# A whole-network kernel in split fp32: one weight piece split per call of the routine, one piece beyond the one in use

## The chip, the cores and the metric

The kernel runs on one core of one Trainium2 chip. The metric is the device time of one execution in microseconds (us), as the median of several runs.

## What is computed

The reference runs two blocks of two layers each over one sequence of 256 tokens with 1024 channels, all in fp32. What matters here is that every layer is a chain of a norm and large matrix products:

```python
def rmsnorm(x, g):
    y = xf * lax.rsqrt(jnp.mean(xf * xf, axis=-1, keepdims=True) + RMS_EPS)
    return (y * g.astype(jnp.float32)).astype(x.dtype)
...
        h = h + mixed
        h = h + squared_relu_mlp(rmsnorm(h, norm_mlp[i]), mlp_w_up[i], mlp_w_down[i])
        ple_gate = jax.nn.sigmoid(rmsnorm(h, norm_ple[i]) @ ple_w_gate[i])
        h = h + ple_gate * (p[i].astype(h.dtype) @ ple_w_proj[i])
    return rmsnorm(h, norm_final)
...
        h = h + 0.5 * _swiglu(_rmsnorm(h, ffn1_norm[layer]), ffn1_w_in[layer], ffn1_w_out[layer])
        u = _rmsnorm(h, mix_norm[layer])
...
        h = h + 0.5 * _swiglu(_rmsnorm(h, ffn2_norm[layer]), ffn2_w_in[layer], ffn2_w_out[layer])
```

The mixers of the first block are a short convolution (layer 0) and a dilated attention (layer 1); those of the second are an S5 state space mixer (layer 0) and a sparse attention with three branches (layer 1), whose keys and values come from one projection (kv) after layer 0. The PLE is the gated term with `ple_w_gate`.

## The kernel before

**Weights.** All large weights are cut into 292 pieces, used in one fixed order (`PLAN`). A piece is 128 x 2048 fp32, 1 MB: either 256 columns of a matrix with 1024 rows ("cols") or 256 rows of one with 1024 columns ("rows"). Twelve of them belong to S5 and are not split. The products have to be more exact than a single pass gives, so each weight and each activation is split into a high part (rounded to the format fp32r) and a low remainder, and a product is three matmuls, hi·hi, lo·hi and hi·lo (`mm3`, L362, L363, L364). A piece is 48 matmuls of 128 x 256.

**Splitting.** `split` takes the next pieces in order. For each it opens two pairs of half tiles (`split_open`), and for each half (128 x 1024) ACT writes the high part whi (L289) and DVE the remainder wlo = raw − whi (L290):

```python
            nc.scalar.activation(hi.t[c], rc, AF.Copy)
            nc.vector.tensor_sub(lo.t[c], rc, hi.t[c].bitcast(F32))
```

The tiles lie in rings: three raw pieces, six halves of whi and six of wlo, so three pieces of each. SP starts the load of a raw piece as soon as the ring lets it.

**Who asks for splits.** `piece()` is called once for each piece that is used, number i. Its `fetch` asks for all pieces below i + 3 to be split (`ahead`), within a cap, and for loads up to i + 6. While a norm is pending, the fetch is kept for later:

```python
        if 0 < len(self.todo) < 4 and self.n_split >= i + 2:
            self.late.append(lambda: self.behind(fetch))
        else:
            fetch()
```

**Norms.** The rows of a layer's input are not scaled before the product; the product is scaled behind it by R, a reciprocal root that is the same for all channels of a token. So the first pieces of a stage run while R is still being made: sums of squares on TensorE (`norm_ssq`, L513), rmean on DVE (L523), the power on GpSimd (rcol, L503), dg on GpSimd (L534), a matmul that spreads it over the partitions (L537), and R, a copy by ACT (L539). `norm_at` puts these steps into `todo`, and `norm_step`, called after every second k of a piece, takes one; when the list is empty, everything in `late` is issued, the kept fetches in order behind what was issued on each engine up to then (`behind`). After R the first outputs are scaled: L544 on DVE (e), then in the ffn stages silu on ACT (L882), a scaling on GpSimd (L883), the product with the second half on DVE (L887), and its own split into hh and hl (L438, L439) for the down product. An ffn copies its very first product out of the accumulator on ACT (L875), before R is there. In PSUM there are three accumulators "acc", four "big" and one "misc".

**The order on the engines.** The kernel's text is not the order of execution: a scheduler with a simulated time line orders the instructions of each engine, within the dependencies, the rings and the places where `in_order` forbids it. Each engine then works through its list in that order.

**S5.** `n_split` jumps over the twelve S5 pieces, three pieces are split ahead of time by `split_open(3)`, and at the end of the first update `split(self.n_use + 2)` (L1319) asks for the pieces that follow.

Of the kernel before, what the change touches and what calls it, by code (L numbers as in the profile page):

```python
# [132 lines left out]
PLAN = plan()  # L133
# [89 lines left out]
class Ker:  # L223
# [17 lines left out]
    def load(self, i):  # L241
        nc = self.nc
        while self.n_load < min(i, len(PLAN)):
# [22 lines left out]
            self.raw[n] = t  # L266
            self.n_load += 1

    def split(self, i):
        while self.n_split < min(i, len(PLAN)):  # L270
            todo = self.split_open(1)
            for c in range(2):
                self.split_half(todo, c)
# [896 lines left out]
    def s5(self, upd):  # L1170
# [112 lines left out]
        def presplit(c):  # L1283
            with self.in_order():
                if c == 0:
                    split.extend(self.split_open(3))
                self.split_half(split, c)
# [25 lines left out]
        def upd2(j):  # L1313
            if j == 0:
                accs.extend(self.cols_open("s5_w_glu_2", 0, (256 * i, 256 * i + 128), ahead=3 - i) for i in range(3))
                for ks in (range(4), range(4, 8)):
                    for a in accs:
                        self.cols_part(x, a, ks)
                self.split(self.n_use + 2)  # L1319
            elif j == 1:  # L1320
                a = self.cols_open("s5_w_glu_2", 0, (768, 896))
                self.cols_part(x, a, range(8))
                accs.append(a)
            s = bp.tile([128, 2, S], F32, name="sZ")
            ac.activation(s, accs[j][0], AF.Sigmoid)
            v.tensor_tensor(s, s, Y[0][:, 2 * j:2 * j + 2], op=OP.mult)
            v.tensor_tensor(self.h[j], self.h[j], s, op=OP.add)

        self.cap = len(PLAN)
        return self.norm_feed(upd2, ("ffn2_norm_2", 0))  # L1330


# [562 lines left out]
```

## Time and profile before

| | |
|---|---|
| median of 3 runs | 1885.36 us (1885.01 to 1886.57) |
| the profiled execution | 1886.62 us |
| its span, first to last instruction | 1884.8 us |
| mean granted clock of TensorE | 0.984 |
| TensorE (PE) busy | 1826.6 us, 97% of the span |
| VectorE (DVE) busy | 1292.8 us, 69% |
| ScalarE (ACT) busy | 956.5 us, 51% |
| GpSimd (POOL) busy | 465.3 us, 25% |
| mean transfer rate | 183 GB/s |

Busy time says how much an engine works, not whether somebody waits for it. The waits of an engine say that: which instruction stood idle, and which instruction of another engine ended the wait. The granted clock tells at what share of its full speed TensorE ran in a stretch.

### The profile page before, as it was taken

Reading aid. Unit: us, or ns where it says so; the run is one execution under the profiler, and the core shown is the slowest. Engines: PE = TensorE matmul, PEld = TensorE weight load, DVE = VectorE, ACT = ScalarE, POOL = GpSimd, SP = SyncE. Lnnn points to the kernel's source line nnn. Section 1 sums busy time; section 2 is a strip of 40 time slices with the busy share of each in tenths; the row PEclk is TensorE's granted clock in tenths of the full one; section 3 lists DMA queues with packets and bytes.
Section 4 is the critical chain, followed back from the end, with each engine's and each line's share of the span. In section 5 each row is a group of like instructions: output and inputs, shape, how many; then the busy total and the mean of one; then the engine's idle time right before and its main releaser. Section 6 shows DMA issues by size and latency. Waiting matters only on the chain.

```text
span 1884.8 us, 36094 instructions
## 1 busy us (share of the span) xinstructions
PE 1826.6 (97%) x15242; PEld 1800.5 (96%) x15242; DVE 1292.8 (69%) x1647; ACT 956.5 (51%) x1438; POOL 465.3 (25%) x391
## 2 busy tenths in 40 slices
PE   8999999899999999998999889999999999999999
PEld 8999999899999999998999888999999999899998
DVE  6879987787777788767655585555686556775554
ACT  4455556454445555556444364444565445764442
POOL 2110012655664332211101211110153113421110
PEclk9999999899999999999999989999999999899999
DMA  6565666443343476665555845755455553344452
GB/s 229 205 211 190 218 206 203 149 164 136 134 157 135 175 252 232 224 195 208 201 191 182 284 190 177 242 181 187 162 183 198 179 189 101 56 165 179 179 180 88
DMA packets 80657, 344.72 MB, mean 183 GB/s; under 512 B 8214, under 2 KB 34570, under 8 KB 44656
## 3 DMA queue, kind: packets, MB, share of 16 engines
q1 hardware_dynamic: 79344, 339.33, 51.4%
q0 software_dynamic: 1008, 2.91, 0.5%
q8 instruction: 119, 1.95, 0.4%
q14 instruction: 42, 0.34, 0.1%
q10 hardware_dynamic: 144, 0.20, 0.0%
HBM read 328.73 MB, written 17.86 MB: 184 GB/s over the span
## 4 chain that ended last, share of the span: by engine, by line
PE 77%; DVE 8%; POOL 5%; issue 4%; ACT 3%; DMA 2%; SPq 0%; POOLq 0%; ACTq 0%; DVEq 0%
PE acc L364 15%; PE acc L363 15%; PE acc L362 15%; PE big L364 8%; PE big L363 8%; PE big L362 8%; DVE wlo L290 3%; POOL qkt L767 2%; POOL qks L764 2%; ACT whi L289 1%; POOL qkc L766 1%; PE acc L1720 1%; DMA bias<-zb 1%; DMA s5wi<-wi 1%; ACT qh L438 1%
## 5 line engine op out<-in xcount | busy, mean ns | idle before, releaser
L290 DVE TENSOR_TENSOR wlo<-raw,whi 128x1024 fp32r<-128x1024 f32 x558 | 709.4, 1282 | 312.4 <-ACT whi L289 309.1
L289 ACT ACTIVATE whi<-raw 128x1024 fp32r<-128x1024 f32 x558 | 581.2, 1056 | 540.5 <-PE acc L363 279.6
L362 PE MATMUL acc<-xh,whi 128*128 128x256 f32 x2096 | 597.0, 286 | 10.5 <-ACT xh L441 3.6
L364 PE MATMUL acc<-xh,wlo 128*128 128x256 f32 x2096 | 597.3, 286 | 5.3 <-DVE wlo L439 3.1
L363 PE MATMUL acc<-xl,whi 128*128 128x256 f32 x2096 | 596.3, 285 | 1.9 <-DVE xl L442 1.8
L362 PEld LDWEIGHTS acc<-xh,whi 128*128 128x128 f32 x2096 | 404.7, 193 | 13.1 <-ACT xh L441 3.8
L364 PEld LDWEIGHTS acc<-xh,wlo 128*128 128x128 f32 x2096 | 404.9, 193 | 7.7 <-DVE wlo L439 3.9
L363 PEld LDWEIGHTS acc<-xl,whi 128*128 128x128 f32 x2096 | 405.1, 193 | 2.6 <-DVE xl L442 2.0
L363 PE MATMUL big<-hl,whi 128*128 128x256 f32 x1216 | 344.1, 284 | 0.0
L364 PE MATMUL big<-hh,wlo 128*128 128x256 f32 x1216 | 342.9, 284 | 0.0
L362 PE MATMUL big<-hh,whi 128*128 128x256 f32 x1216 | 342.4, 283 | 0.0
L363 PEld LDWEIGHTS big<-hl,whi 128*128 128x128 f32 x1216 | 232.8, 191 | 1.1 <-issue 1.1
L364 PEld LDWEIGHTS big<-hh,wlo 128*128 128x128 f32 x1216 | 232.0, 191 | 1.5 <-issue 1.5
L362 PEld LDWEIGHTS big<-hh,whi 128*128 128x128 f32 x1216 | 232.2, 191 | 0.2 <-issue 0.2
L883 POOL TENSOR_TENSOR e<-e,R 128x512 f32<-128x512 f32 x44 | 74.0, 1682 | 554.0 <-ACT e L882 544.9
L363 PE MATMUL acc<-yl,whi 128*128 128x256 f32 x720 | 203.2, 284 | 0.7 <-DVE yl L488 0.6
L364 PE MATMUL acc<-yh,wlo 128*128 128x256 f32 x720 | 203.1, 284 | 0.0
L362 PE MATMUL acc<-yh,whi 128*128 128x256 f32 x720 | 202.3, 285 | 0.4 <-ACT yh L474 0.4
L363 PEld LDWEIGHTS acc<-yl,whi 128*128 128x128 f32 x720 | 138.0, 192 | 1.3 <-DVE yl L488 1.3
L362 PEld LDWEIGHTS acc<-yh,whi 128*128 128x128 f32 x720 | 137.5, 193 | 1.0 <-ACT yh L474 0.6
L364 PEld LDWEIGHTS acc<-yh,wlo 128*128 128x128 f32 x720 | 138.1, 192 | 0.1
L482 POOL TENSOR_TENSOR sq<-sq,sqt 128x512 f32<-128x512 f32 x27 | 42.0, 1554 | 138.5 <-ACT sqt L481 137.9
(440 smaller groups left out, 2609.9 us busy)
## 6 DMA issues: line engine op xcount, KB each, us to landing
raw<-in_wst SPq DMA_DIRECT2D x277, 1024.0 KB, 4.9
s5wo<-b SPq DMA_DIRECT2D x8, 512.0 KB, 5.8
s5wi<-wi SPq DMA_DIRECT2D x16, 256.0 KB, 5.2
s5to<-s5k SPq DMA_DIRECT2D x32, 128.0 KB, 3.9
bias<-zb SPq DMA_DIRECT2D x16, 256.0 KB, 4.6
cbt<-zb SPq DMA_DIRECT2D x4, 900.0 KB, 8.6
raw<-s5to SPq DMA_DIRECT2D x6, 512.0 KB, 6.1
raw<-in_wst SPq DMA_DIRECT2D x4, 512.0 KB, 8.0
```

Of the source, the lines that this page charges most:

```text
L289: nc.scalar.activation(hi.t[c], rc, AF.Copy)
L290: nc.vector.tensor_sub(lo.t[c], rc, hi.t[c].bitcast(F32))
L362: mm(out, lh, rh, start=first, stop=False, skip_group_check=True)
L363: mm(out, lh, rl, start=False, stop=False, skip_group_check=True)
L364: mm(out, ll, rh, start=False, stop=last, skip_group_check=True)
L438: nc.scalar.activation(hi, src, AF.Copy)
L482: nc.gpsimd.tensor_tensor(self.sq, self.sq, s, op=OP.add)
L764: nc.gpsimd.tensor_tensor(s, s, bc(self.rS), op=OP.mult)
L766: nc.gpsimd.tensor_tensor(c, t[:32], bc(self.rC), op=OP.mult)
L767: nc.gpsimd.tensor_tensor(t[:32], c, s, op=OP.add)
L883: nc.gpsimd.tensor_tensor(T[i], T[i], self.bc2(self.R), op=OP.mult)
L1720: nc.tensor.matmul(o[:, dst], w, t[lp][e][:, b, src], start=False, stop=(b == 1 and kb == 1 and i == 2), skip_group_check=True)
```

## The change

`split` takes one piece per call at most, in place of all pieces up to the number asked for; both halves of that piece are still split in the call. And the request behind the first S5 update is for one piece beyond `n_use` in place of two. All requests stay as they are otherwise; since a stage begins with one call per piece, the split pieces are one fewer in the program at a given call than before, i + 2 after call i in place of i + 3, and the condition with which `piece()` keeps a fetch for later reads that number. A blank line is added as well, so the change's line numbers stand one above those of before from L269 on.

```diff
@@ -266,8 +266,9 @@
             self.raw[n] = t
             self.n_load += 1
 
+
     def split(self, i):
-        while self.n_split < min(i, len(PLAN)):
+        if self.n_split < min(i, len(PLAN)):
             todo = self.split_open(1)
             for c in range(2):
                 self.split_half(todo, c)
@@ -1316,7 +1317,7 @@
                 for ks in (range(4), range(4, 8)):
                     for a in accs:
                         self.cols_part(x, a, ks)
-                self.split(self.n_use + 2)
+                self.split(self.n_use + 1)
             elif j == 1:
                 a = self.cols_open("s5_w_glu_2", 0, (768, 896))
                 self.cols_part(x, a, range(8))
```

How that moves instructions is seen in three places. First DVE in the PLE of layer 0, from the step rmean of its norm on; e are the products scaled by R, four of them, pp the projection they are added to. Before:

```order
L523 TENSOR_SCALAR rmean<-misc 128x2
L544 TENSOR_TENSOR e_3978<-acc,R 128x512
L544 TENSOR_TENSOR e_4047<-acc,R 128x512
L290 TENSOR_TENSOR wlo<-raw,whi 128x1024 x5
L544 TENSOR_TENSOR e_4060<-acc,R 128x512
L705 TENSOR_TENSOR e_4049<-e_4049,pp_3555 128x512
L706 TENSOR_TENSOR h_72<-h_72,e_3980 128x512
L290 TENSOR_TENSOR wlo<-raw,whi 128x1024
L706 TENSOR_TENSOR h_73<-h_73,e_4049 128x512
L290 TENSOR_TENSOR wlo<-raw,whi 128x1024
L544 TENSOR_TENSOR e_4073<-acc,R 128x512
```

and now:

```order
L291 TENSOR_TENSOR wlo<-raw,whi 128x1024 x2
L524 TENSOR_SCALAR rmean<-misc 128x2
L291 TENSOR_TENSOR wlo<-raw,whi 128x1024 x2
L545 TENSOR_TENSOR e_3970<-acc,R 128x512
L545 TENSOR_TENSOR e_4039<-acc,R 128x512
L291 TENSOR_TENSOR wlo<-raw,whi 128x1024
L706 TENSOR_TENSOR e_4041<-e_4041,pp_3547 128x512
L707 TENSOR_TENSOR h_72<-h_72,e_3972 128x512
L545 TENSOR_TENSOR e_4052<-acc,R 128x512
L707 TENSOR_TENSOR h_73<-h_73,e_4041 128x512
L291 TENSOR_TENSOR wlo<-raw,whi 128x1024
```

Of the block of five halves behind the first two scaled products, one is left; the others stand ahead of them.

Second ACT at the start of the attention: sqt are the squares for the norm, R its result, qh the high part of a query. Before:

```order
L481 ACTIVATE sqt<-h_75 128x512
L433 ACT_TABLE_LOAD
L433 ACTIVATE tab<-ones 128x1
L539 ACTIVATE R<-misc 128x256
L438 ACTIVATE qh_4207<-qkt 128x512
L289 ACTIVATE whi<-raw 128x1024 x6
L438 ACTIVATE qh_4265<-qkt 128x512
```

and now:

```order
L290 ACTIVATE whi<-raw 128x1024 x2
L475 ACTIVATE xh_3751<-h_75,small 128x256
L475 ACTIVATE xh_3752<-h_75,small 128x256
L482 ACTIVATE sqt<-h_75 128x512
L434 ACT_TABLE_LOAD
L434 ACTIVATE tab<-ones 128x1
L290 ACTIVATE whi<-raw 128x1024 x3
L540 ACTIVATE R<-misc 128x256
L290 ACTIVATE whi<-raw 128x1024 x2
L439 ACTIVATE qh_4209<-qkt 128x512
```

Three halves stand between the table and R and two between R and the first query, where there were none.

Third ACT behind the final norm of the first block, at the start of ffn1 of layer 0. Before:

```order
L433 ACT_TABLE_LOAD
L433 ACTIVATE tab<-ones 128x1
L875 ACTIVATE e_10435<-acc 128x512
L539 ACTIVATE R<-misc 128x256
L882 ACTIVATE e_10458<-e_10456 128x512
L289 ACTIVATE whi<-raw 128x1024 x6
L882 ACTIVATE e_10589<-e_10587 128x512
L438 ACTIVATE hh<-e_10458 128x512
L539 ACTIVATE R_10485<-misc 128x256
```

and now:

```order
L434 ACT_TABLE_LOAD
L434 ACTIVATE tab<-ones 128x1
L290 ACTIVATE whi<-raw 128x1024
L876 ACTIVATE e_10427<-acc 128x512
L290 ACTIVATE whi<-raw 128x1024 x4
L540 ACTIVATE R<-misc 128x256
L883 ACTIVATE e_10460<-e_10458 128x512
L883 ACTIVATE e_10581<-e_10579 128x512
L439 ACTIVATE hh<-e_10460 128x512
L439 ACTIVATE hh<-e_10581 128x512
```

The six halves behind the first silu are gone from there; five stand ahead of R, and both silu follow R at once.

## Rows read from the trace of the kernel before

**Rows 1.** Waits of TensorE: total us, times, longest.
```profile
PE big L362 <- ACT whi L289: 5.7, 3, 3.1
...
PE acc L362 <- ACT xh L441: 3.6, 1, 3.6
...
PE acc L362 <- ACT whi L289: 2.6, 2, 2.3
PE acc L362 <- DVE e L544: 2.4, 1, 2.4
...
PE acc L364 <- DVE wlo L290: 2.1, 2, 1.1
...
PE acc L363 <- DVE xl L442: 1.8, 1, 1.8
...
PE big L364 <- DVE wlo L290: 1.0, 1, 1.0
```
**Rows 2.** Windows: us, busy of PE, PEld, DVE, ACT, POOL, PEclk, DMA, GB/s.
```profile
328.00:340.00 12.00, 9.22 (x61) 8.69 (x60) 11.81 (x18) 8.24 (x17) 4.15 (x2) 0.86 0.77 275
348.00:364.00 16.00, 11.87 (x73) 11.14 (x72) 11.86 (x14) 7.21 (x9) 11.79 (x8) 0.79 0.16 56
855.00:872.00 17.00, 11.58 (x76) 11.18 (x76) 16.89 (x27) 12.07 (x28) 0.12 (x1) 0.80 0.59 211
1138.00:1150.00 12.00, 8.73 (x57) 8.26 (x57) 7.96 (x8) 7.74 (x10) 2.65 (x3) 0.86 0.19 67
1336.00:1348.00 12.00, 9.43 (x62) 8.93 (x61) 8.69 (x9) 6.06 (x7) 1.54 (x4) 0.86 0.37 117
1181.00:1187.00 6.00, 6.00 (x52) 6.00 (x52) 3.38 (x4) 2.64 (x3) 2.14 (x2) 1.00 0.56 201
```
**Rows 3.** Waits of ACT: total us, times, longest.
```profile
ACT whi L289 <- PE acc L363: 279.6, 170, 2.7
ACT whi L289 <- PE big L363: 122.0, 86, 2.7
...
ACT R L539 <- PE misc L537: 76.6, 10, 10.6
```
**Rows 4.** Time line of ACT, attention start: start, us, instruction, [idle before <-releaser].
```profile
348.84 0.38 ACT L539 ACTIVATE R<-misc 128x256 f32<-128x256 f32 x1 [7.13 <-PE misc L537]
353.98 0.63 ACT L438 ACTIVATE qh<-qkt 128x512 fp32r<-128x512 f32 x1 [4.75 <-POOL qkt L767]
354.51 5.78 ACT L289 ACTIVATE whi<-raw 128x1024 fp32r<-128x1024 f32 x6
```
**Rows 5.** Time line of ACT behind R, at ffn2 of layer 0 and at kv.
```profile
1142.25 5.77 ACT L289 ACTIVATE whi<-raw 128x1024 fp32r<-128x1024 f32 x6
...
1338.85 5.78 ACT L289 ACTIVATE whi<-raw 128x1024 fp32r<-128x1024 f32 x6
```
**Rows 6.** Time line of DVE in the PLE of layer 0.
```profile
318.76 1.29 DVE L544 TENSOR_TENSOR e<-acc,R 128x512 f32<-128x512 f32 x2 [4.87 <-ACT R L539]
319.97 6.87 DVE L290 TENSOR_TENSOR wlo<-raw,whi 128x1024 fp32r<-128x1024 f32 x5
...
331.43 0.68 DVE L544 TENSOR_TENSOR e<-acc,R 128x512 f32<-128x512 f32 x1
```
**Rows 7.** Page, part 5: busy us, mean ns of one, idle before and releaser.
```profile
L290 DVE TENSOR_TENSOR wlo<-raw,whi 128x1024 fp32r<-128x1024 f32 x558 | 709.4, 1282 | 312.4 <-ACT whi L289 309.1
L289 ACT ACTIVATE whi<-raw 128x1024 fp32r<-128x1024 f32 x558 | 581.2, 1056 | 540.5 <-PE acc L363 279.6
```
**Rows 8.** Time lines of PE and POOL, ffn1 of layer 0.
```profile
880.65 0.59 PE L537 MATMUL misc<-dg,ones 128*128 128x256 f32 x2
...
883.13 1.28 POOL L883 TENSOR_TENSOR e<-e,R 128x512 f32<-128x512 f32 x1 [4.94 <-ACT e L882]
```
**Rows 9.** Group of L534 (ns min/median/max), and time lines of POOL and DVE there.
```profile
L534 POOL TENSOR_TENSOR dg<-cst,rcol x11: 612/613/1161, 23.7 to 1697.1; 128x256 f32<-128x256 f32 x11
...
885.15 0.97 POOL L534 TENSOR_TENSOR dg<-cst,rcol 128x256 f32<-128x256 f32 x1
...
884.39 1.25 DVE L290 TENSOR_TENSOR wlo<-raw,whi 128x1024 fp32r<-128x1024 f32 x1
```

## The prediction

> **What bounds the kernel now.** I read the waits of TensorE first. TensorE is busy nearly all the span, so a change pays only by closing its idle stretches, or by opening new ones. The seven rows that bear on splits and norms [rows 1] hold 5.7 + 3.6 + 2.6 + 2.4 + 2.1 + 1.8 + 1.0 = 19.2 us. Where each falls I took from the windows [rows 2], one per place with the granted clock beside it:
>
> - PLE of layer 0 (332 us): the 2.4 on DVE's L544.
> - attention start (355 us): 3.1 on whi, then the 1.0 on wlo.
> - final norm into ffn1 of layer 0 (860 to 886 us): 3.6 on ACT's xh and 1.8 on DVE's xl, then 0.3 on whi and 1.1 on wlo.
> - ffn2 of layer 0 (1143 us): 2.3 on whi, 1.0 on wlo.
> - kv projection (1340 us): 5.7 − 3.1 = 2.6 on whi.
>
> Each place pays twice. After the idle time the granted clock is lower: 0.86, 0.79, 0.80, 0.86 and 0.86 in these windows, against 1.00 in an undisturbed one [rows 2]; 1.00 is the level of 2.4 GHz, and the windows mix it with 1.2. The shortfall, window times (1 − clock), is time lost at the lower level: 12 × 0.14 = 1.7, 16 × 0.21 = 3.4, 17 × 0.20 = 3.4, 1.7 and 1.7 us.
>
> All five have one cause, seen on ACT and DVE next. While a norm is pending, `piece` puts the fetch of later weights behind R (L539). So ACT stands idle before R, 76.6 us at 10 norms [rows 3], and right after it, or after the first output, issues a whole block of splits. At the attention start it idles 7.13 us before R and 4.75 before qh, and only then runs six halves in 5.78 us [rows 4]; TensorE waits for the first. At ffn2 and at kv six halves follow R in the same way [rows 5]. At the PLE the block stands on DVE: five halves, 6.87 us, ahead of the L544 that TensorE waits for [rows 6]; before the final norm the same five-half block delays the h from which xh and xl come.
>
> **The change part by part.** *One piece per call.* At the start of a stage the lead in the program falls from two pieces beyond the one in use to one. No instruction is added or removed; the counts on all five engines are equal. In the long ffn stretches the order on ACT and DVE reads the same before and after, since the buffers set it: whi waits 279.6 us for TensorE to free a half while acc matmuls run and 122.0 while big ones do [rows 3]. Cost there: zero. The cover is those 401.6 us of waiting; were it gone, one half (1.06 us on ACT, 1.28 on DVE [rows 7]) would be exposed per piece.
>
> *The condition.* With one piece of lead, `n_split >= i + 2` is false when a norm is pending, so the fetch is issued at once. This is the part that moves time. In the order, two to seven halves that stood behind R now stand ahead of it at the norms, on ACT and on DVE, with the SP loads that their freed raw buffers trigger. The idle time that they enter is there: 76.6 us in 10 norms, 7.7 each; seven halves take 7 × 1.06 = 7.4 on ACT. By place:
>
> - PLE: from the first pair of L544 to the fourth one it took 331.43 − 318.76 = 12.7 us [rows 6]. Now two halves run between rmean and that pair, in DVE's idle 4.87, and from pair to fourth stand three halves (1.2 each back to back) and eleven operations of 0.4 to 0.65: some 10.1, so 2.6 sooner; the wait was 2.4. Gain 2.4 + 1.7 = 4.1.
> - attention start: five halves stand before qh where none did. Gain 3.1 + 1.0 + 3.4 = 7.5; less 0.5, as part of the slow stretch lies in the second wait, and less 1, since norm and first head's transposes stand 24 and 49 matmuls later in the order and something of this is late. Gain 6.0.
> - ffn2: four halves ahead of R. Gain 2.3 + 1.0 + 1.7 = 5.0.
> - kv: six halves ahead of R. Gain 2.6 + 1.7 = 4.3.
> - final norm: gross 3.6 + 1.8 + 0.3 + 1.1 + 3.4 = 10.2, less 0.9 for the slow stretch inside the second wait: 9.3. But here the order takes something back. L537, which makes R, stands 192 matmuls into the stage, where it stood at 123. At 0.12 us a matmul (52 of them touch a busy window of 6.00 us, [rows 2]) that is 8.3 us more work ahead of it. The next piece needs the acc buffer of the second one, which L887 frees after R. From L537 to L883 takes 883.13 − 880.65 = 2.48 us, L883 1.28 [rows 8], L887 some 0.7 (as the other DVE operations on 512 columns): 4.5. TensorE stands for about 4.3 of it, and I add 1.7 for the clock, as at the other places with 2 to 3 us. Gain 9.3 − 6.0 = 3.3.
>
> *S5.* `n_use + 1` in place of 2 at L1319 moves the split of one glu piece a little later; the order there shows swaps of neighbours. Bounds: two halves earlier or later, −2.3 to +2.3 us; I take 0, since the waits of S5 in the trace are on other names. The interleave of background work in both mlps shifts too; TensorE has no idle time on splits there. Bounds −2 to +2, taken as 0.
>
> *A cost that the rows price.* Splits ahead of R run beside the GpSimd operations that make R. dg (L534) took 0.61 us in the median, but 0.97 at 885.15, where a wlo split ran until 885.64 [rows 9]. I add nothing at four places, since TensorE does not wait for R there. The Trainium skill (SBUF — State Buffer, SBUF: two separate sides) says that DVE and GpSimd share a pair of ports, which a DVE operation with two SBUF inputs, as a wlo split is, locks for its whole length against a GpSimd operation that reads SBUF; the stretched dg agrees. By that rule rcol and dg could each wait out one split, and the gain at the final norm would be some 2.6 us less by the durations above.
>
> Sum: 4.1 + 6.0 + 3.3 + 5.0 + 4.3 = 22.7 us. Profiled execution 1886.62 − 22.7 = 1863.9; it stands 1.3 above the median of 1885.36, so by the median 1862.7. I forecast **1863**.
>
> **The rivals.**
>
> 1. *Half the gain.* The splits come early, but the attention start and the final norm stay held by the chain of R (rmean, rcol, dg, L537, R, then L544 and GpSimd). For it: at both, L537 is later in the order. Against: 24 matmuls are 2.9 us, and the whi that TensorE waited for needs no R. Left are PLE, ffn2 and kv: 13.4 us, 1886.6 − 13.4 = 1873, by the median 1872.
>
> 2. *No change.* The wait is for TensorE to free a half, so a split issued earlier only waits earlier. For it: the 401.6 us of such waits [rows 3]. Against: at the five places ACT idles for R or qh, not for a buffer. 1885.
>
> 3. *Slower: R is held by the splits ahead of it.* ACT takes instructions in order. If a half ahead of R waits for a buffer that matmuls behind the norm free, R waits with it, and all that scales by R. It decides where more halves stand ahead of R than are free. The price is the final norm's, 4.3 + 1.7 = 6.0 us, at 10 norms [rows 3], 60, less 22.7 kept: +37, 1923. For it: up to seven halves ahead of R against a ring of six. Against: right after R six halves run without a gap [rows 5], so their buffers were free by then, and a half ahead of R could hold it only until that point. The Trainium skill (TensorE: Matmul & The Clock Gate, Architectural detail) says that the queues of ACT and DVE are strictly first in, first out, by which a blocked half would hold R; the rows agree in so far as ACT's rows stand in the order's sequence.
>
> 4. *It does not do what it says.* The words speak of half a piece; the code still splits both halves, one piece per call. That by itself changes no number above. But after the nsa mixer the program's lead is used up, each call splitting its own piece. If ACT ran in that order, about 37 pieces would each expose 1.06 + 1.28 us, 86 us: 1971. Against: the order rows there are the same as before.
>
> **How the numbers follow.** Forecast 0.55, half the gain 0.27, no change 0.09, R held 0.07, lead used up 0.02. The first two make faster 0.82; same is 0.09, slower 0.09. A measurement tells 0.2%, 3.8 us, from no change. Range: its low end is the forecast less the 6.0 taken back at the final norm, less 2 to 3 for S5 and the mlps: 1854. Its high end is the half gain, 1872, plus one new wait of 6.0 and the 2 of the mlps: 1880. What lies outside is no change and the slower cases, 0.18.
>
> **What would show it.** Right: ACT's whi runs ahead of R and the idle time before R is well under 76.6 us; the rows whi → big and whi → acc (5.7, 2.6) nearly vanish; windows at 332, 355, 1143 and 1340 us have clock over 0.95; one new wait of 3 to 5 us near 880 us on DVE's L887. Wrong: TensorE waits on R, on qh or on L544 where it waited on whi, or the whi waits reappear in stretches where the order did not change. The forecast fails if clock losses stay though the waits go, or if new waits open in the mlps.

## The result and the profile after

The changed kernel took 1860.43 us in the median of 4 runs (1859.66 to 1861.85), against 1885.96 us before (4 runs); the ratio is 0.9865, 95% interval 0.9848 to 0.9882, so 25.5 us or 1.35% less. The forecast was 1863.

First the waits of TensorE after, in the view of [rows 1] (total us, times, longest; the change's lines stand one higher):

```profile
PE big L818 <- ACT p L813: 8.2, 3, 2.9
PE big L1229 <- DVE sX L1265: 6.6, 2, 5.5
...
PE acc L363 <- ACT e L883: 3.1, 1, 3.1
...
PE acc L363 <- DVE e L654: 2.3, 1, 2.3
...
PE big L364 <- DVE ql L440: 1.4, 1, 1.4
```

None of the seven rows of [rows 1] is left: not one wait on a whi or wlo that `split` makes, on xh or xl of the final norm, or on L544 of the PLE. Those 19.2 us are gone whole. (The very first piece is split elsewhere, in `first_feed`; TensorE still waits for it, 4.6 us before and 5.1 now.) Three smaller waits are new: e (L883) behind the final norm, e (L654) at the start of the second mlp, ql in the attention. Two more rows need a look. One is p, in the heads of the attention; before, it read:

```profile
PE big L817 <- ACT p L812: 7.6, 4, 2.8
```

It is 0.6 us longer now: a wait of 2.5 us at head 0 (380 us) is new, and one of 2.8 at 452 us of before is gone. The other, sX in S5, was 3.2 us with 2.6 as the longest, beside 3.2 us at the same line on issue (waits for which the profile shows no releaser), of which 0.4 are left; the waits in S5 come to 12.1 us before and 12.4 now. All waits of TensorE add up to some 53 us before and 40 now, so about half of the 25.5 us is idle time. The other half is the clock: its mean rose from 0.984 to 0.991, and span times (1 − clock) fell from 30.2 to 16.7 us.

Next the windows of the five places in the profile after, each with the same columns as [rows 2], and then three with a wait in them (the final norm's R, the second mlp, head 0 of the attention):

```profile
322.00:336.00 14.00, 14.00 (x119) 14.00 (x118) 14.00 (x19) 10.11 (x17) 2.82 (x2) 1.00 0.49 168
342.00:358.00 16.00, 16.00 (x134) 15.95 (x134) 12.45 (x17) 7.67 (x10) 11.60 (x7) 1.00 0.48 156
840.00:857.00 17.00, 17.00 (x143) 16.94 (x142) 17.00 (x25) 14.12 (x28) 2.14 (x1) 1.00 0.49 181
866.00:882.00 16.00, 12.85 (x92) 12.43 (x91) 10.08 (x15) 7.30 (x11) 6.42 (x6) 0.89 0.82 337
1125.00:1137.00 12.00, 12.00 (x101) 11.95 (x100) 10.24 (x12) 6.88 (x10) 4.67 (x5) 1.00 0.63 234
1317.00:1329.00 12.00, 12.00 (x101) 11.95 (x101) 8.95 (x9) 4.87 (x6) 2.81 (x6) 1.00 0.70 261
630.00:640.00 10.00, 7.68 (x52) 7.51 (x51) 10.00 (x10) 4.28 (x6) 4.87 (x3) 0.83 0.29 105
375.00:385.00 10.00, 7.52 (x52) 7.31 (x51) 6.54 (x9) 6.84 (x12) 5.85 (x5) 0.83 0.27 96
```

Where [rows 2] had 9 to 12 us of work in 12 to 17 us at a clock of 0.79 to 0.86, TensorE now works without a stop at 1.00, the 2.4 GHz level, in five of the windows. Only the stretch behind the final norm (0.89) still shows a shortfall there, 16 × 0.11 = 1.8 us, and the two last windows show 1.7 each; that of head 0 stands in place of one at 452 us, where the clock was 0.79 from 450 to 458 us before.

The cause shows on ACT. Its waits (the view of [rows 3]):

```profile
ACT whi L290 <- PE acc L364: 346.6, 213, 3.6
ACT whi L290 <- PE big L364: 141.7, 95, 3.1
...
ACT R L540 <- PE misc L538: 8.7, 8, 2.0
```

ACT idled 76.6 us ahead of ten R, and now 8.7 ahead of eight; at the others R was issued with no wait of its own. The waits of whi for a free half grew by 67.0 + 19.7 us instead: ACT now idles with the splits already next in its list, so a half is written as soon as it is free. The time line of ACT at the attention start (the view of [rows 4]):

```profile
340.46 1.06 ACT L290 ACTIVATE whi<-raw 128x1024 fp32r<-128x1024 f32 x1 [1.86 <-PE acc L364]
341.77 2.01 ACT L290 ACTIVATE whi<-raw 128x1024 fp32r<-128x1024 f32 x2 [0.26 <-PE acc L364]
344.84 0.38 ACT L540 ACTIVATE R<-misc 128x256 f32<-128x256 f32 x1 [1.06 <-PE misc L538]
345.61 1.06 ACT L290 ACTIVATE whi<-raw 128x1024 fp32r<-128x1024 f32 x1 [0.39 <-PE acc L364]
348.48 1.06 ACT L290 ACTIVATE whi<-raw 128x1024 fp32r<-128x1024 f32 x1 [1.80 <-PE big L364]
351.97 0.63 ACT L439 ACTIVATE qh<-qkt 128x512 fp32r<-128x512 f32 x1 [2.43 <-POOL qkt L768]
```

Five halves run between the table load and the first qh, where [rows 4] has none and then six at once.

### The profile page after: what moved, and what is told of

Same layout as the page of the kernel before. It is cut to its first block, busy times and chain, and to the rows that moved or that the text cites. A ratio compares the mean times of both kernels' runs of the same rounds, so it can differ in the third digit from the quotient of the medians.

```text
span 1859.3 us, 36126 instructions
## 1 busy us (share of the span) xinstructions
PE 1814.1 (98%) x15242; PEld 1790.5 (96%) x15242; DVE 1292.1 (69%) x1647; ACT 961.5 (52%) x1438; POOL 457.5 (25%) x391
```

## The experiments

The theory: the condition at the norms, that is, fetches no longer kept behind R, is the whole effect, and each place is a term of its own. The rival: the smaller lead, one piece per call, helps by itself.

**No kept fetch, everything else as before.**

```diff
-        if 0 < len(self.todo) < 4 and self.n_split >= i + 2:
+        if False:
```

> The kernel before, with its loop and its lead of two pieces kept, but no fetch is ever kept for behind R. Theory (the condition at the norms is the whole effect): the halves ahead of R are those of the changed kernel, so the time is too, 1860 us within 4; the waits of TensorE on whi, xh and xl at the five places are gone, and the new waits at the start of the second mlp (2.3 us) and behind the final norm (3.2 us) are there. Rival (the smaller lead itself, one piece per call, is what helps, since it leaves buffers and queues freer): nearly no change, 1882 to 1888 us. Half and half would lie at 1873.

Measured: 1861.32 us (4 runs), ratio 0.9868 (0.9852 to 0.9884). With the loop and the lead of two pieces as before, the gain is the same as the change's. The lead of one piece by itself is worth nothing that these runs can tell, with intervals of some 3 us either way. The run's waits of TensorE have the final norm's row again, with no row on whi of `split` (L289) or on e at the second mlp (L653 there):

```profile
PE acc L362 <- ACT e L882: 3.1, 1, 3.1
```

The 2.3 us at the second mlp that the expectation put here was absent; only 0.6 us stood there, of another kind. So that wait belongs to the changed kernel's order at that place; the condition alone does not bring it.

**One piece per call, but fetches kept again.**

```diff
-        if 0 < len(self.todo) < 4 and self.n_split >= i + 2:
+        if 0 < len(self.todo) < 4 and self.n_split >= i + 1:
```

(on top of the change)

> The changed kernel, one piece per call, with the condition loosened by one so that fetches are kept for behind R again. Eight of ten R have two or more halves fewer ahead of them than the kernel before had. Theory: the gain is lost or more than lost, 1884 to 1895 us, with waits of TensorE on whi behind R at most norms, 2 to 4 us each plus 1.7 of lower clock. Rival (the smaller lead helps by itself): it stays at 1860 to 1866 us.

Measured: 1915.34 us, ratio 1.016 (1.0143 to 1.0177), beyond the range expected: 55 us over the changed kernel. Its waits of TensorE, in the view of [rows 1]:

```profile
PE acc L363 <- ACT whi L290: 22.4, 8, 6.8
...
PE acc L365 <- DVE wlo L291: 7.0, 8, 1.7
...
PE big L363 <- ACT whi L290: 4.8, 1, 4.8
```

and ACT at the attention start there:

```profile
357.32 0.38 ACT L540 ACTIVATE R<-misc 128x256 f32<-128x256 f32 x1 [3.65 <-PE misc L538]
362.40 0.63 ACT L439 ACTIVATE qh<-qkt 128x512 fp32r<-128x512 f32 x1 [4.70 <-POOL qkt L768]
362.94 5.77 ACT L290 ACTIVATE whi<-raw 128x1024 fp32r<-128x1024 f32 x6
```

This is [rows 4] with a piece less in hand: the same block of six behind qh, and TensorE waits 6.8 us for it where it waited 3.1. Nearly every norm has such a wait now, 9 on whi with 27.2 us in all, and the mean clock is 0.978 (0.984 before). With the fetches kept, a smaller lead is harmful; the change gains only through the condition that its lead happens to switch off.

**Only the late norms, and only the early ones** (the kernel before; d is the piece's distance from the first S5 piece).

```diff
-        if 0 < len(self.todo) < 4 and self.n_split >= i + 2:
+        if 0 < len(self.todo) < 4 and self.n_split >= i + 2 and d < 0:
```

> The kernel before; fetches are not kept only from S5 on (norms of ffn2 of layer 0, kv, ffn1 and nsa of layer 1). Theory (each place is a sum of its own): ffn2 and kv give their 5.0 and 4.3, so 1886 - 9.3 = 1877 us; if the 3.9 us that the changed kernel gained in the nsa stage come from its norm too, 1873. Rival (what is gained at one place is lost again at a later one, or the gain in nsa is chance): 1880 or more, or 1877 with the nsa stage as before.

Measured: 1875.15 us, ratio 0.9945 (0.9929 to 0.9961), 10.0 less than the 1885.12 of its runs of before. In the profile the waits at ffn2 and kv are gone, and those of the PLE, of the attention start and of the final norm are there.

The other half:

```diff
-        if 0 < len(self.todo) < 4 and self.n_split >= i + 2:
+        if 0 < len(self.todo) < 4 and self.n_split >= i + 2 and d >= 0:
```

> The kernel before; fetches are not kept only ahead of S5. Theory: what the changed kernel's trace shows up to S5: PLE and first mlp 6.7 us sooner, attention 5.6, second mlp 4.0 later, final norm 5.4 sooner, so 1886 - 13.7 = 1872 us. With the run of the late norms alone the two gains add up to that of the changed kernel within 4 us. Rival (the places are coupled by loads and buffers): the two do not add up.

Measured: 1867.57 us, ratio 0.9908 (0.9893 to 0.9924), 17.6 less. The rows on whi that are left are those of kv and of ffn2:

```profile
PE big L362 <- ACT whi L289: 2.6, 2, 1.4
PE acc L362 <- ACT whi L289: 1.9, 1, 1.9
```

10.0 + 17.6 = 27.6 against 25.5 of the changed kernel and 23.8 of the run without any kept fetch: the sum holds within the 4 us stated. The early part gave 4 more than its 13.7, in which the 4.0 lost at the second mlp were counted; that loss does not occur in this order either.

**Single places.** Fetches are not kept at the PLE of layer 0 alone:

```diff
-        if 0 < len(self.todo) < 4 and self.n_split >= i + 2:
+        if 0 < len(self.todo) < 4 and self.n_split >= i + 2 and not 49 <= i < 53:
```

> The kernel before; fetches are not kept at one place only, the PLE of layer 0. Theory: the wait of 2.4 us on L544 and its 1.7 of clock go, and nothing else changes: 1885 - 4.1 = 1881 us, with the 3.1 and 1.0 at the attention start as before. Rival (the splits done earlier run on, so the attention start's waits go as well, 7.5): 1874. Rival (only the place of the block on ACT matters, DVE's L544 stays late): 1885.

Measured: 1882.82 us (10 runs), ratio 0.9981 (0.9971 to 0.9991), 3.0 less. L544's wait of 2.4 us is gone. But the waits on whi in the attention were not "as before":

```profile
PE big L362 <- ACT whi L289: 7.9, 3, 5.3
```

5.7 and 3.1 had stood there [rows 1]. TensorE came to the attention start earlier, and as ACT still did its block of splits only behind qh, it waited 2.2 us longer there. Of the 2.4 us almost all moved to the next place; what stayed is about the clock and some small waits.

The attention start alone:

```diff
-        if 0 < len(self.todo) < 4 and self.n_split >= i + 2:
+        if 0 < len(self.todo) < 4 and self.n_split >= i + 2 and not 53 <= i < 57:
```

> The kernel before; fetches are not kept at one place only, the attention start. Theory: the 3.1 and 1.0 us and 3.4 of clock there go, the 2.4 at the PLE stays; the products of head 0 come later by some 1 to 4 us, as the changed kernel's wait of 2.5 on p and 1.4 on ql showed: 1885 - 7 + 3 = 1881 us, at the best 1878. Rival (the norm's later place takes all of it back): 1885.

Measured: 1875.96 us, ratio 0.9943 (0.9928 to 0.9958), 9.8 less; better than the 1878 named as best. Its profile has neither the 3.1 nor the 1.0 us, and 2.5 us on p and 0.4 on ql in their place, as expected. From the end of the PLE to the end of the attention (346 to 634 us of before, taken between the same matmuls) that profile is 7.1 us shorter than the profile of before and 6.2 shorter than the second one of that order (below), close to the 6.0 of the prediction. The rest of the 9.8 is not at this place: its profile also lacks the lower clock in the nsa stage, the sparse attention (see below). The two places together give 12.8.

**Can the final norm's new wait be avoided?** No kept fetch, but for the final norm:

```diff
-        if 0 < len(self.todo) < 4 and self.n_split >= i + 2:
+        if 0 < len(self.todo) < 4 and self.n_split >= i + 2 and 130 <= i < 134:
```

> As the run without any kept fetch, but at the final norm of the first block (ffn1 of layer 0) the fetches are kept behind R as before. There 266 halves stand ahead of R in place of 274, and L537 stands 48 matmuls earlier. Theory (at this place the splits ahead of R, and L537 being late, cost a wait of 3.1 us and 1.7 of clock; the waits of 3.6 and 1.8 before it belonged to the PLE's block of splits, not to this norm's): the 3.1 goes, the 0.3 and 1.1 on whi and wlo behind R come back, and the clock keeps or loses 1.7: between 1.7 less and 3.4 less than that run, 1858 to 1860 us. Rival (the 3.6 and 1.8 come back with the kept fetch, as they fell at this norm): 1864 to 1866.

Measured: 1860.3 us, ratio 0.9863 (0.9848 to 0.9877), the same as without it (1861.32). ACT at this norm and the wait of TensorE that it causes:

```profile
864.66 0.38 ACT L539 ACTIVATE R<-misc 128x256 f32<-128x256 f32 x1 [3.11 <-PE misc L537]
865.80 0.63 ACT L882 ACTIVATE e<-e 128x512 f32<-128x512 f32 x1 [0.76 <-DVE e L544]
866.34 5.77 ACT L289 ACTIVATE whi<-raw 128x1024 fp32r<-128x1024 f32 x6
```

```profile
PE acc L362 <- ACT whi L289: 2.8, 1, 2.8
```

The wait on e (L882) went, as the theory has it, and the 3.6 and 1.8 on xh and xl did not come back, so those belonged to the block of splits in the PLE of layer 1. But the 0.3 on whi came back as 2.8: TensorE arrives earlier, and the kept block is later relative to it. That part of the expectation failed; one wait was exchanged for another of the same size.

With the fetches kept at the second mlp's norm as well:

```diff
-        if 0 < len(self.todo) < 4 and self.n_split >= i + 2:
+        if 0 < len(self.todo) < 4 and self.n_split >= i + 2 and (93 <= i < 96 or 130 <= i < 134):
```

> As the run before this one, with the fetches kept behind R also at the second mlp's norm. Theory: that norm had no wait before, and none in the run without kept fetches beyond 0.6 us; the 2.3 us of the changed kernel there came from background work that DVE's order put ahead of the first scaled products, not from the splits. So the time is the one of the run before this within 2 us. Rival (splits ahead of R cost that norm too): 2 to 4 us less.

Measured: 1858.72 us, ratio 0.9859 (0.9844 to 0.9873): within 2 us of the run above, and not to be told from the changed kernel. No version measured beats it beyond the intervals.

**Each line of the change alone.** One piece per call with `n_use + 2` kept at L1319 (on top of the change):

```diff
-                self.split(self.n_use + 1)
+                self.split(self.n_use + 2)
```

> The change without its second part: one piece per call, and still n_use + 2 behind the first S5 update. Every engine's order is that of the changed kernel row for row, so theory and rival agree on the time, 1860 us within 2; if the second part mattered in another way, 2 us off or more. It is also a second profile of the same order: theory (what fell away in the nsa stage, 5.1 us of clock, is not the change's) has that stage vary between the two profiles by one such stretch, or at least allows it; rival (it belongs to the changed order) has the same waits and the full clock there again, at 1570 to 1590 us.

and the kernel before with `n_use + 1` there:

```diff
-                self.split(self.n_use + 2)
+                self.split(self.n_use + 1)
```

> The kernel before with the second part of the change alone, n_use + 1 behind the first S5 update. Every engine's order is that of the kernel before, so 1885 us within 2, and a second profile of that order: the waits at the five places are there again within 0.3 us each, with 1.7 or 3.4 us of clock; the nsa stage shows the lower clock again (10.2 us of it) if that belongs to the order, and may not if it varies by execution.

Measured: 1857.67 us, ratio 0.9853 (0.9836 to 0.9869), and 1885.03 us (10 runs), ratio 0.9998 (0.9989 to 1.0007). The second part of the change does nothing, as the unchanged order said. The first run lies 2.8 us under the changed kernel's median where 2 were allowed, with intervals that overlap. Both serve as second profiles of the two orders. Before, with that line (the view of [rows 1]):

```profile
PE big L362 <- ACT whi L289: 5.7, 3, 3.1
PE acc L362 <- ACT xh L441: 3.8, 1, 3.8
...
PE acc L362 <- ACT whi L289: 2.6, 2, 2.3
PE acc L362 <- DVE e L544: 2.4, 1, 2.4
PE acc L364 <- DVE wlo L290: 2.1, 2, 1.1
```

The waits at the five places repeat to 0.2 us in these rows; xl's 1.8 was 1.2. These waits are set by the order, not by the execution. The clock behind them is not, and there the expectation failed: in the second profile the granted clock is 0.72 at the PLE (328 to 340 us) and 1.00 at kv (1338 to 1350 us), where the first has 0.86 at both [rows 2], behind the same waits. So the PLE cost 3.4 us of clock in place of 1.7, and kv none. In the nsa stage the execution matters most: over the same 55 us the granted clock was, in the kernel before, in its second profile, in the changed kernel and in its second profile:

```profile
1565.00:1620.00 55.00, 52.22 (x367) 48.34 (x366) 34.23 (x92) 31.96 (x91) 19.99 (x30) 0.91 0.30 73
```

```profile
1565.00:1620.00 55.00, 50.69 (x384) 46.81 (x383) 36.68 (x96) 32.40 (x93) 20.88 (x30) 1.00 0.31 79
```

```profile
1565.00:1620.00 55.00, 50.66 (x380) 45.89 (x378) 42.42 (x122) 39.62 (x145) 23.60 (x49) 1.00 0.33 59
```

```profile
1565.00:1620.00 55.00, 51.44 (x363) 46.63 (x360) 41.77 (x119) 38.83 (x143) 23.66 (x49) 0.94 0.33 59
```

0.91 and 1.00 for one order, 1.00 and 0.94 for the other. The 5 us that one comparison of profiles would give to the change here (55 × 0.09) are a matter of the execution.

## Why the prediction was right

The direction, the place of the effect and its size held: 22.7 us were summed, 25.5 measured. That the sum came so near is in part luck. The two orders have two profiles each; between the same matmuls (counted in TensorE's order) of a profile of before and one of the changed order, PLE and attention start together gave 11.3 to 13.3 us (the prediction has 10.1), the final norm 4.3 to 5.0 (3.3), ffn2 5.2 to 5.3 (5.0) and kv 3.1 to 4.6 (4.3). Four terms that were 0 in the sum, or not in it, moved by as much and nearly cancel: the first mlp gained 2.5, the second lost 1.3 to 3.6, S5 lost 0.3 to 3.7, and nsa lies between 2.2 lost and 3.1 gained. By its steps:

- *Lead of one piece, cost zero in the long stretches.* Right, and shown: no wait on a half made by `split` is left anywhere, and the run without kept fetches but with the lead of two is as fast. The experiments' rival, that the lead itself helps, fell.
- *The condition moves the splits ahead of R.* Right; within some 3 us it is the whole effect, shown from both sides, 1861 without kept fetches and 1915 with the lead of one and the fetches kept.
- *ffn2 5.0 and kv 4.3.* Both places now run at 1.00 without a wait; the late norms alone gave 10.0 against 9.3. The 1.7 of clock that the sum took at kv was there in one of the two profiles of before.
- *PLE 4.1.* DVE's fourth scaled product came 329.54 − 317.59 = 12.0 us after the first pair, not 10.1 (the changed kernel's time line of DVE), and TensorE still did not wait for it:

```profile
317.59 1.28 DVE L545 TENSOR_TENSOR e<-acc,R 128x512 f32<-128x512 f32 x2
...
329.54 0.68 DVE L545 TENSOR_TENSOR e<-acc,R 128x512 f32<-128x512 f32 x1
```

  Behind the pair it came 0.7 us sooner, not 2.6. TensorE's own order helped, which the prediction does not name: before, TensorE did two matmuls of the next stage and then stood until that product was done; now 28 of them start ahead of its end at 330.22 us (the trace of PE, from 326.88 us on). The gain of this place alone was 3.0, since most of the wait passes on to the attention start unless that place is mended too.
- *Attention start, 7.5 less 1.5.* The waits went. The "less 1" for head 0 was somewhat small: 1.4 on ql and, at 375 to 385 us, 2.5 on p with 1.7 of clock, against one such wait on p that went at 452 us. The place alone gave 9.8, of which 6 to 7 lie at the place itself; the rest lies in other stages such as nsa, where the two profiles of before differ by 3.2 us.
- *Final norm, 4.3 + 1.7 taken back.* The wait is there, of 3.1 and 1.8 of clock, but it ends with the first silu (L883), ahead of GpSimd's scaling, not at the end of the chain on L887. (The silu ended last before TensorE went on; the second of the two L545, which reads an acc, ended 0.06 us earlier, so the view does not tell which of them it was.) The place held; the chain was taken too long, and splits held it, which the prediction did not count (below). The term was over-sized by 1.2.
- *The mlps, ±2, taken as 0.* This term held in its sum and failed in its parts. The second mlp got a wait of 2.3 us on L654, 1.7 of clock in one profile; a new wait in the mlps was one of the prediction's own signs of failing. There DVE's order has background work of S5 (L1083, 2.4 us, and L1085, 2.2) and one split ahead of the first pair of products, which begins 5.0 us behind R's end; without kept fetches, where the wait is absent, it begins 3.2 us behind R's end, with less of that work and no split ahead of it. Two waits on background work in the first mlp, 1.8 us in all, went in turn; the changed profile has none there.
- *S5, ±2.3, taken as 0.* The request behind the first update changed nothing, as its run alone showed. But the longest wait in S5, on sX, is 5.5 us in place of 2.6, and it is so in the run without kept fetches and in that of the attention start alone as well, both with the request as before. So the order in S5 shifts with the fetches at the norms, at about the same idle time in all; why it shifts stays open.

Half the gain (rival 1) fell with the windows at 1.00. No change (rival 2) fell too, though its premise is visible: the splits do wait earlier, 488.3 us in place of 401.6; but that is waiting by ACT, with TensorE served in time. Rival 4 did not occur; there is no wait on a half made by `split`, in the last 37 pieces or elsewhere.

Rival 3, R held by a split ahead of it, occurs in small, and at the final norm it is part of the new wait. TensorE, ACT and DVE there:

```profile
871.54 0.59 PE L538 MATMUL misc<-dg,ones 128*128 128x256 f32 x2
```

```profile
871.62 1.06 ACT L290 ACTIVATE whi<-raw 128x1024 fp32r<-128x1024 f32 x1 [1.82 <-PE acc L364]
872.58 0.37 ACT L540 ACTIVATE R<-misc 128x256 f32<-128x256 f32 x1
```

```profile
872.71 1.22 DVE L291 TENSOR_TENSOR wlo<-raw,whi 128x1024 fp32r<-128x1024 f32 x1 [1.65 <-ACT whi L290]
873.85 0.68 DVE L545 TENSOR_TENSOR e<-e,R 128x512 f32<-128x512 f32 x1
```

L538 ended at 872.13, but R began only at 872.58, behind a half that had waited for its buffer and ran to 872.68. R ended at 872.95, but L545 began only at 873.85, behind the wlo of that half. That is 0.4 and 0.9 us, at most, of the 3.1. No run takes this part away alone: the run with the fetches kept there takes these splits away, but sets another block behind the silu.

On the GpSimd chain of R: at the same norm rcol took 1.61 us beside wlo splits, where the same operation took 0.69 further on.

```profile
867.67 1.61 POOL L504 TENSOR_TENSOR rcol<-rq,mhalf 128x2 f32<-128x2 f32 x1 [24.84 <-DVE rq L939]
869.36 0.61 POOL L535 TENSOR_TENSOR dg<-cst,rcol 128x256 f32<-128x256 f32 x1
...
876.51 0.69 POOL L504 TENSOR_TENSOR rcol<-rmean,mhalf 128x2 f32<-128x2 f32 x1
```

The Trainium skill (SBUF — State Buffer, SBUF: two separate sides) would let each of the two operations wait out one split, by the prediction's estimate 2.6 us in all; here the trace agrees for rcol, by 0.9 us, and dg ran free, with no split running when it began. Those 0.9 us cost nothing: dg was done at 869.97, and TensorE came to L538 only at 871.54.

## What to carry to other kernels

Work that needs nothing from a serial chain (here the next weights' splits) should stand ahead of the chain's last step in each engine's order, in the time in which that engine idles; put behind it, it arrives as a block just when the chain's result starts the next consumer. Only so much of it should stand there as does not hold the chain itself, as it did by 1.3 us at the final norm. And look for what a changed number switches on or off: the lead of one piece cost 30 us with the fetches kept and nothing without, so the same edit is a gain or a loss by a condition elsewhere. A wait closed at one place passes on to the next place with the same fault, so such places are mended together and their gains counted together.

## What had not been expected

A wait's loss is not only its own length, and the rest is not fixed. The wait of 2.3 us at the second mlp was in both profiles of the changed order, but the granted clock behind it was 0.83 in one window of 10 us (above) and 1.00 in the other profile's:

```profile
627.00:637.00 10.00, 7.68 (x64) 7.51 (x63) 10.00 (x10) 4.65 (x7) 5.36 (x3) 1.00 0.31 113
374.00:384.00 10.00, 7.51 (x51) 7.31 (x50) 6.56 (x9) 6.74 (x12) 5.85 (x5) 0.83 0.22 84
```

Head 0's wait of 2.5 us, the second line, had 0.83 in both, and in the two profiles of before the PLE cost 1.7 and 3.4 us of clock, kv 1.7 and none. So 1.7 us is what such a wait may cost on top, not what it must; with the 5 us in nsa this is the spread within which a sum over places from one profile can be compared with a measured difference.
